# VectorE and ScalarE as loops over one ring of rows, in a fused linear layer with a low-rank part

## The chip, the cores and the metric

The kernel runs on one core of a Trainium2 chip. The metric is the device time of one execution in microseconds (us), the median of several runs. A separate execution was profiled; its trace gives the durations below.

## The reference

`x` is 16 x 2048 rows of 256 float32 values, 32768 rows in all. The result is a linear layer plus a scaled low-rank one:

```python
x_flat = x.reshape(-1, in_dim)              # 32768 x 256
y = x_flat @ W                              # W: 256 x 256
lora_out = ((x_flat @ lora_A) * lora_E) @ lora_B   # rank 16
y = y + scale * lora_out                    # float32, 32768 x 256
```

Input and output have 33.5 MB each.

## The kernel before

**Weights.** The low-rank part is folded into the weights once: `weff = W + A diag(E) B * scale`, in bf16. This takes two small transposes (L194), two small products (L198), and four short VectorE instructions (L127 to L138). After that, the work is one 256 x 256 product for every row of `x`.

**Chunks.** The rows are cut by `PLAN` into chunks; a plan entry `b` means `b` rows on each of the 128 partitions. Before, there are nine chunks: 16, seven times 32, and 16. A chunk of 32 is a DMA of 4 MB, in which each partition gets one run of 32 KB. Six buffers `xy` of 32 rows each hold chunks; the result is written over the input in the same buffer and stored from there. Together they take 192 KB of each partition.

**Steps.** Each chunk is worked on in steps of `Q = 4` rows a partition, 64 steps in all:

- VectorE rounds four rows to bf16 (`xb`, L146).
- TensorE transposes them with eight transposes into PSUM (`ps_xt`, L176).
- VectorE copies the transposed block to SBUF (`xt`, L155).
- TensorE multiplies: eight matmuls into PSUM (`ps_y`, L184).
- ScalarE copies the result to `xy` in float32 (L163). At the end of a chunk a drain (L165) adds one to the semaphore `s_rdy`.

`xb`, `xt`, `ps_xt` and `ps_y` have two buffers each. VectorE and TensorE run one step ahead: the rounding and the transposes of step k+1 come before the copy and the products of step k. TensorE's program is a loop of two steps already; its waits take semaphores down by one (`take`, L170). The programs of VectorE and ScalarE are written out for all 64 steps, with a wait for `s_in[i]` on VectorE at the first step of chunk i.

**Transfers.** All large transfers are issued by SP, in one queue (q1), and are split over 16 DMA engines. The order is written out by hand: the weights, six loads (`LEAD`), then for each chunk a wait for `s_rdy` and its store (L109). After the store of chunk 2, `AFTER` puts the loads of chunks 6, 7 and 8 (L102), each behind a wait until the store from the same buffer has landed (`s_out`). At the end SP waits for the last stores.

Of the kernel before, what the change touches and what calls it, by code (L numbers as in the profile page):

```python
# [6 lines left out]

PLAN = [16] + [32] * 7 + [16]  # L10

ROWS, SLOTS = 32, 6

LEAD = 6
AFTER = {2: [6, 7, 8]}

Q = 4


@with_exitstack  # L20
def kernel(
    ctx: ExitStack,
    tc: tile.TileContext,
    x: bass.AP,
    W: bass.AP,
    lora_A: bass.AP,
    lora_B: bass.AP,
    lora_E: bass.AP,
    scale: bass.AP,
    out: bass.AP,  # L30
):
    nc = tc.nc
    P = 128
    FP32 = mybir.dt.float32
    BF16 = mybir.dt.bfloat16

    x_flat = x.flatten_outer_dims()
    out_flat = out.flatten_outer_dims()
    N, K = x_flat.shape
    M = out_flat.shape[1]  # L40
    R = lora_B.shape[0]
    KC = K // P
    CHUNKS = len(PLAN)
    assert K == M and sum(PLAN) * P == N and all(b % Q == 0 for b in PLAN)

    def sbuf(name, shape, dt):
        return ctx.enter_context(nc.sbuf_tensor(name, shape, dt))

    def psum(name, shape, dt):
        return ctx.enter_context(nc.psum_tensor(name, shape, dt))  # L50

    xy = [sbuf(f"xy{s}", [P, ROWS, K], FP32) for s in range(SLOTS)]
    xb = [sbuf(f"xb{s}", [P, Q, K], BF16) for s in range(2)]
    xt = [sbuf(f"xt{s}", [P, Q, KC, P], BF16) for s in range(2)]
    w_sb = sbuf("w_sb", [P, KC, M], FP32)
    a_sb = sbuf("a_sb", [P, KC, R], FP32)
    b_sb = sbuf("b_sb", [R, M], FP32)
    e_sb = sbuf("e_sb", [R, 1], FP32)
    b_bf = sbuf("b_bf", [R, M], BF16)
    ate = sbuf("ate", [R, KC, P], BF16)  # L60
    weff = sbuf("weff", [P, KC, M], BF16)
    ident = sbuf("ident", [P, P], FP32)
    ident_bf = sbuf("ident_bf", [P, P], BF16)

    ps_xt = [psum(f"ps_xt{s}", [P, Q, KC, P], BF16) for s in range(2)]
    ps_y = [psum(f"ps_y{s}", [P, Q, M], FP32) for s in range(2)]
    ps_at = psum("ps_at", [P, KC, P], FP32)
    ps_aeb = psum("ps_aeb", [P, KC, M], FP32)

    sem = tc.alloc_semaphore  # L70
    s_w, s_a, s_b, s_e = sem("s_w"), sem("s_a"), sem("s_b"), sem("s_e")
    s_in = [sem(f"s_in{i}") for i in range(CHUNKS)]

    again = CHUNKS - SLOTS
    s_out = [sem(f"s_out{i}") for i in range(again + 1)]
    s_id = sem("s_id")
    s_lora = sem("s_lora")
    s_lpe = sem("s_lpe")
    s_xb = sem("s_xb")
    s_t = sem("s_t")  # L80
    s_xt = sem("s_xt")
    s_p = sem("s_p")
    s_y = sem("s_y")
    s_rdy = sem("s_rdy")

    starts = [sum(PLAN[:i]) * P for i in range(CHUNKS)]

    def rows_of(flat, i):
        b, r0 = PLAN[i], starts[i]
        return flat[r0:r0 + b * P, :].rearrange("(p b) k -> p b k", b=b)  # L90


    steps = [(i, r) for i, b in enumerate(PLAN) for r in range(0, b, Q)]
    n = len(steps)
    assert n % 2 == 0

    with tc.tile_critical(sync_engine=mybir.EngineType.SP, no_gpsimd_drain=True):  # L97
        sp, pe, dve, act, pool = nc.sync, nc.tensor, nc.vector, nc.scalar, nc.gpsimd


        def load(i):
            sp.dma_start(out=xy[i % SLOTS][:, :PLAN[i], :], in_=rows_of(x_flat, i)).then_inc(s_in[i], 16)  # L102

        sp.dma_start(out=w_sb[:], in_=W.rearrange("(c p) m -> p c m", p=P)).then_inc(s_w, 16)
        for i in range(LEAD):
            load(i)
        for i in range(CHUNKS):
            sp.wait_ge(s_rdy, i + 1)
            sp.dma_start(out=rows_of(out_flat, i), in_=xy[i % SLOTS][:, :PLAN[i], :]).then_inc(s_out[min(i, again)], 16)  # L109
            for later in AFTER.get(i, []):  # L110
                if later >= SLOTS:
                    sp.wait_ge(s_out[later - SLOTS], 16)
                load(later)
        for i in range(len(s_out) - 1):
            sp.wait_ge(s_out[i], 16)


        pool.memset(ident[:], 0.0).then_inc(s_id, 1)  # L118
        pool.wait_ge(s_id, 1)
        pool.affine_select(  # L120
            out=ident[:], in_=ident[:], compare_op=mybir.AluOpType.not_equal, fill=1.0,
            base=0, pattern=[[-1, P]], channel_multiplier=1,
        ).then_inc(s_id, 1)


        dve.wait_ge(s_id, 2)
        dve.tensor_copy(out=ident_bf[:], in_=ident[:]).then_inc(s_lora, 1)  # L127
        dve.wait_ge(s_b, 16)
        dve.tensor_copy(out=b_bf[:], in_=b_sb[:]).then_inc(s_lora, 1)  # L129
        dve.wait_ge(s_e, 16)  # L130
        dve.wait_ge(s_lpe, 1)
        dve.tensor_scalar(  # L132
            out=ate[:], in0=ps_at[:R, :, :], scalar1=e_sb[:], scalar2=float(scale),
            op0=mybir.AluOpType.mult, op1=mybir.AluOpType.mult,
        ).then_inc(s_lora, 1)
        dve.wait_ge(s_w, 16)
        dve.wait_ge(s_lpe, 2)
        dve.tensor_add(out=weff[:], in0=w_sb[:], in1=ps_aeb[:]).then_inc(s_lora, 1)  # L138

        def round_step(k):  # L140
            i, r = steps[k]
            if r == 0:
                dve.wait_ge(s_in[i], 16)
            if k >= 2:
                dve.wait_ge(s_t, k - 1)
            dve.tensor_copy(out=xb[k % 2][:], in_=xy[i % SLOTS][:, r:r + Q, :]).then_inc(s_xb, 1)  # L146

        round_step(0)
        for k in range(n):
            if k + 1 < n:  # L150
                round_step(k + 1)
            dve.wait_ge(s_t, k + 1)
            if k >= 2:
                dve.wait_ge(s_p, k - 1)
            dve.tensor_copy(out=xt[k % 2][:], in_=ps_xt[k % 2][:]).then_inc(s_xt, 1)  # L155


        act.dma_start(out=a_sb[:], in_=lora_A.rearrange("(c p) r -> p c r", p=P)).then_inc(s_a, 16)
        act.dma_start(out=b_sb[:], in_=lora_B).then_inc(s_b, 16)
        act.dma_start(out=e_sb[:], in_=lora_E[:, None]).then_inc(s_e, 16)  # L160
        for k, (i, r) in enumerate(steps):
            act.wait_ge(s_p, k + 1)
            act.copy(out=xy[i % SLOTS][:, r:r + Q, :], in_=ps_y[k % 2][:]).then_inc(s_y, 1)  # L163
            if r + Q == PLAN[i]:
                act.drain().then_inc(s_rdy, 1)  # L165

        def take(s):
            pe.wait_ge(s, 1).then_inc(s, -1)  # L170

        def transposes(k):
            take(s_xb)
            for j in range(Q):
                for c in range(KC):
                    t = pe.transpose(ps_xt[k % 2][:, j, c, :], xb[k % 2][:, j, c * P:(c + 1) * P], ident_bf[:])  # L176
            t.then_inc(s_t, 1)

        def products(k):
            take(s_xt)  # L180
            take(s_y)
            for j in range(Q):
                for c in range(KC):
                    m = pe.matmul(  # L184
                        ps_y[k % 2][:, j, :], xt[k % 2][:, j, c, :], weff[:, c, :],
                        start=(c == 0), stop=(c == KC - 1),
                    )
            m.then_inc(s_p, 1)

        pe.sem_inc(s_y, 2)  # L190
        pe.wait_ge(s_a, 16)
        pe.wait_ge(s_id, 2)
        for c in range(KC):
            t = pe.transpose(ps_at[:R, c, :], a_sb[:, c, :], ident[:])  # L194
        t.then_inc(s_lpe, 1)
        pe.wait_ge(s_lora, 3)
        for c in range(KC):
            m = pe.matmul(ps_aeb[:, c, :], ate[:, c, :], b_bf[:], start=True, stop=True)  # L198
        m.then_inc(s_lpe, 1)
        transposes(0)  # L200
        pe.wait_ge(s_lora, 4)
        with pe.Fori(0, n // 2 - 1):
            transposes(1)
            products(0)
            transposes(0)
            products(1)
        transposes(1)
        products(0)
        products(1)


    with tc.tile_critical(sync_engine=mybir.EngineType.SP, no_gpsimd_drain=True):
        nc.sync.wait_ge(s_out[again], 16 * (CHUNKS - again))
# [34 lines left out]
```

## Time and profile before

| | us |
|---|---|
| median of 3 runs | 165.41 (165.13 to 165.42) |
| the profiled execution's own time | 165.19 |
| its span, first to last instruction | 163.4 |
| TensorE busy | 90.8 |
| VectorE busy | 84.1 |
| ScalarE busy | 66.1 |
| DMA, mean over the span | 413 GB/s |

The profiled execution's time has 1.8 us around its span. The page lists groups of instructions by line, with the total busy time, the mean of one in nanoseconds, and the idle time just before them with what ended it. Times in the trace count from the start of the span. In the list of DMA issues, the time to landing counts from the issue, so it holds the time in the queue too: a store of 4 MB takes 39.5 us at the median. Where the prediction speaks of single packets, these are the trace's records of the DMA engines: when a packet began, how long it took, its size and queue. A landing is the moment at which one of the 16 DMA engines has reported its part of a transfer.

### The profile page before, as it was taken

To read this page: it belongs to the slowest core of one execution; us is meant where nothing else is said; L and a number is where in the kernel's file an instruction comes from. 1 tells how busy PE (TensorE), PEld (TensorE's weight loads), DVE (VectorE), ACT (ScalarE), POOL (GpSimd) and SP (SyncE) were. 2 spreads that over 40 slices of the span, in tenths; PEclk is the share of its full clock that TensorE was granted. 3 is DMA by queue.
4 is the path that set the end of the run, shared out by engine and by line. 5 is a ranking of instruction groups with operands and counts; after the bars stand their busy time and mean duration, and the time that the engine had idled before them with its cause. 6 is when DMAs were issued, how large, how long until landed. Compare 5 with 4: busy or idle time off the path is not lost. (4 is left out here: it accounts for less than half of the span.)

```text
span 163.4 us, 2684 instructions
## 1 busy us (share of the span) xinstructions
PE 90.8 (56%) x1028; PEld 81.6 (50%) x1028; DVE 84.1 (51%) x132; ACT 66.1 (40%) x65; POOL 0.7 (0%) x6
## 2 busy tenths in 40 slices
PE   0169499999999999990000099999992000000000
PEld 0047389999999999980000089999981000000000
DVE  0165299999999999950000169999970000000000
ACT  3002447777777777772000026777774000000000
POOL 1000000000000000000000000000000000000000
PEclk9999999999999999999555559999999755555555
DMA  4999999899999999999999998999999999999990
GB/s 133 421 433 489 393 449 449 385 473 425 403 481 393 385 409 481 393 457 425 433 433 425 441 441 383 465 437 425 425 435 433 441 409 465 417 425 441 409 409 32
DMA packets 3203, 67.43 MB, mean 413 GB/s; under 512 B 624, under 2 KB 896, under 8 KB 896
## 3 DMA queue, kind: packets, MB, share of 16 engines
q1 hardware_dynamic: 2864, 67.37, 96.4%
q10 hardware_dynamic: 336, 0.03, 0.3%
q14 instruction: 3, 0.02, 0.0%
HBM read 33.85 MB, written 33.55 MB: 412 GB/s over the span
## 5 line engine op out<-in xcount | busy, mean ns | idle before, releaser
L163 ACT COPY xy<-ps_y 128x1024 f32<-128x1024 f32 x64 | 64.8, 1013 | 56.2 <-PE ps_y L184 56.2
L184 PE MATMUL ps_y<-weff,xt 128*128 128x256 bf16 x512 | 68.6, 278 | 0.5 <-PEq L170 0.3
L146 DVE CAST xb<-xy 128x1024 bf16<-128x1024 f32 x64 | 43.6, 683 | 24.9 <-DMA xy<-in_x_dram 24.9
L176 PE MATMUL ps_xt<-ident_bf,xb 128*128 128x128 bf16 x512 | 40.9, 226 | 24.7 <-PEq L170 24.7
L184 PEld LDWEIGHTS ps_y<-weff,xt 128*128 128x128 bf16 x512 | 48.4, 100 | 6.4 <-issue 1.1
L176 PEld LDWEIGHTS ps_xt<-ident_bf,xb 128*128 128x128 bf16 x512 | 35.5, 102 | 27.3 <-issue 25.7
L155 DVE COPY xt<-ps_xt 128x1024 bf16<-128x1024 bf16 x64 | 44.2, 691 | 5.4 <-PE ps_xt L176 3.7
L194 PE MATMUL ps_at<-ident,a_sb 128*16 128x128 f32 x2 | 0.6, 402 | 4.1 <-DMA a_sb<-in_lora_A_dram 4.1
L198 PE MATMUL ps_aeb<-b_bf,ate 16*128 16x256 bf16 x2 | 0.6, 404 | 3.6 <-DVE ate L132 3.6
L129 DVE CAST b_bf<-b_sb 16x256 bf16<-16x256 f32 x1 | 0.3, 280 | 3.9 <-DMA b_sb<-in_lora_B_dram 3.9
L163 ACT ACT_TABLE_LOAD x1 | 1.3, 1283 | 2.5 <-issue 2.5
L198 PEld LDWEIGHTS ps_aeb<-b_bf,ate 16*128 16x128 bf16 x2 | 0.1, 106 | 4.1 <-DVE ate L132 4.1
L194 PEld LDWEIGHTS ps_at<-ident,a_sb 128*16 128x16 f32 x2 | 0.1, 94 | 4.1 <-DMA a_sb<-in_lora_A_dram 4.1
L132 DVE TENSOR_SCALAR ate<-ps_at,e_sb 16x256 bf16<-16x256 f32 x1 | 0.5, 472 | 1.6 <-DMA e_sb<-in_lora_E_dram 1.6
L127 DVE CAST ident_bf<-ident 128x128 bf16<-128x128 f32 x1 | 0.2, 227 | 1.7 <-POOL ident L120 1.7
L138 DVE TENSOR_TENSOR weff<-w_sb,ps_aeb 128x512 bf16<-128x512 f32 x1 | 0.7, 687 | 0.8 <-PE ps_aeb L198 0.8
L120 POOL TENSOR_SCALAR_AFFINE_SELECT ident<-ident 128x128 f32<-128x128 f32 x1 | 0.3, 293 | 0.2 <-POOL ident L118 0.2
L118 POOL MEMSET ident<- 128x128 f32 x1 | 0.2, 204 | 0.5 <-SPq L97 0.5
L229 POOL MEMSET const-bfloat16-1.0<- 128x1 bf16 x1 | 0.1, 101 | 0.0
L229 POOL MEMSET const-uint8-127<- 128x1 uint8 x1 | 0.1, 101 | 0.0
L229 POOL MEMSET const-float32-0.0<- 128x1 f32 x1 | 0.1, 98 | 0.2 <-issue 0.2
L229 POOL MEMSET const-float32-1.0<- 128x1 f32 x1 | 0.1, 98 | 0.0
## 6 DMA issues: line engine op xcount, KB each, us to landing
xy<-in_x_dram SPq DMA_DIRECT2D x7, 4096.0 KB, 29.1
out_dram<-xy SPq DMA_DIRECT2D x7, 4096.0 KB, 39.5
xy<-in_x_dram SPq DMA_DIRECT2D x2, 2048.0 KB, 16.3
out_dram<-xy SPq DMA_DIRECT2D x2, 2048.0 KB, 39.3
w_sb<-in_W_dram SPq DMA_DIRECT2D x1, 256.0 KB, 2.9
a_sb<-in_lora_A_dram ACTq DMA_DIRECT2D x1, 16.0 KB, 3.1
b_sb<-in_lora_B_dram ACTq DMA_DIRECT2D x1, 16.0 KB, 4.4
e_sb<-in_lora_E_dram ACTq DMA_DIRECT2D x1, 0.1 KB, 5.7
```

The lines of the kernel that those rows point to most:

```text
L120: pool.affine_select(out=ident[:], in_=ident[:], compare_op=mybir.AluOpType.not_equal, fill=1.0, base=0, pattern=[[-1, P]], channel_multip ...
L129: dve.tensor_copy(out=b_bf[:], in_=b_sb[:]).then_inc(s_lora, 1)
L132: dve.tensor_scalar(out=ate[:], in0=ps_at[:R, :, :], scalar1=e_sb[:], scalar2=float(scale), op0=mybir.AluOpType.mult, op1=mybir.AluOpType. ...
L138: dve.tensor_add(out=weff[:], in0=w_sb[:], in1=ps_aeb[:]).then_inc(s_lora, 1)
L146: dve.tensor_copy(out=xb[k % 2][:], in_=xy[i % SLOTS][:, r:r + Q, :]).then_inc(s_xb, 1)
L155: dve.tensor_copy(out=xt[k % 2][:], in_=ps_xt[k % 2][:]).then_inc(s_xt, 1)
L163: act.copy(out=xy[i % SLOTS][:, r:r + Q, :], in_=ps_y[k % 2][:]).then_inc(s_y, 1)
L176: t = pe.transpose(ps_xt[k % 2][:, j, c, :], xb[k % 2][:, j, c * P:(c + 1) * P], ident_bf[:])
L184: m = pe.matmul(ps_y[k % 2][:, j, :], xt[k % 2][:, j, c, :], weff[:, c, :], start=(c == 0), stop=(c == KC - 1),)
L194: t = pe.transpose(ps_at[:R, c, :], a_sb[:, c, :], ident[:])
L198: m = pe.matmul(ps_aeb[:, c, :], ate[:, c, :], b_bf[:], start=True, stop=True)
L229: nc = _bacc.Bacc("TRN2", target_bir_lowering=False, num_devices=1)
```

## The change

- `xy` is one tensor of 192 rows (`RING`). A view `xy_turns` divides it into turns of eight rows (`TURN`), and each turn into two steps of four.
- VectorE's and ScalarE's programs are loops over turns. They pass over the ring twice: 24 turns in a first loop, the remaining 8 in a second one, with the ring's rows addressed by a register.
- VectorE no longer waits for `s_in`. GpSimd waits for each load in turn and adds its four turns to the semaphore `s_ld`; VectorE takes one for each turn.
- Within a turn the order is: both roundings, then both copies on VectorE; both transposes, then both products on TensorE. The step ahead across turns is gone, and TensorE's loop has 32 turns with nothing before or after it.
- ScalarE drains once a turn, and SP's waits for `s_rdy` count turns.
- The plan is eight chunks of 32 rows. Six loads go first; after the store of chunk 1 come the loads of chunks 6 and 7, which wait for the stores of the chunks whose rows they take (0 and 1).

The diff, cut to its core:

```diff
-PLAN = [16] + [32] * 7 + [16]
-ROWS, SLOTS = 32, 6
+PLAN = [32] * 8
+RING = 192
 LEAD = 6
-AFTER = {2: [6, 7, 8]}
+AFTER = {1: [6, 7]}
 Q = 4
+TURN = 2 * Q
...
-    xy = [sbuf(f"xy{s}", [P, ROWS, K], FP32) for s in range(SLOTS)]
+    xy = sbuf("xy", [P, RING, K], FP32)
+    xy_turns = xy[:].rearrange("p (t k q) d -> p t k (q d)", k=2, q=Q)
...
+    passes = [RING, sum(PLAN) - RING]
+    turns = sum(PLAN) // TURN
...
         for i in range(CHUNKS):
-            sp.wait_ge(s_rdy, i + 1)
-            sp.dma_start(out=rows_of(out_flat, i), in_=xy[i % SLOTS][:, :PLAN[i], :]).then_inc(s_out[min(i, again)], 16)
+            sp.wait_ge(s_rdy, (starts[i] + PLAN[i]) // TURN)
+            sp.dma_start(out=rows_of(out_flat, i), in_=ring_of(i)).then_inc(s_out[min(i, again)], 16)
             for later in AFTER.get(i, []):
-                if later >= SLOTS:
-                    sp.wait_ge(s_out[later - SLOTS], 16)
+                sp.wait_ge(s_out[owner[later]], 16)
                 load(later)
...
+        for i in range(CHUNKS):
+            pool.wait_ge(s_in[i], 16).then_inc(s_ld, PLAN[i] // TURN)
+
+        def take(engine, s):
+            engine.wait_ge(s, 1).then_inc(s, -1)
...
-        round_step(0)
-        for k in range(n):
-            if k + 1 < n:
-                round_step(k + 1)
-            dve.wait_ge(s_t, k + 1)
-            if k >= 2:
-                dve.wait_ge(s_p, k - 1)
-            dve.tensor_copy(out=xt[k % 2][:], in_=ps_xt[k % 2][:]).then_inc(s_xt, 1)
+        for rows in passes:
+            with dve.Fori(0, rows // TURN) as turn:
+                take(dve, s_ld)
+                for k in range(2):
+                    dve.tensor_copy(out=xb[k][:], in_=xy_turns[:, bass.ds(turn, 1), k, :]).then_inc(s_xb, 1)
+                for k in range(2):
+                    take(dve, s_t)
+                    dve.tensor_copy(out=xt[k][:], in_=ps_xt[k][:]).then_inc(s_xt, 1)
...
-        for k, (i, r) in enumerate(steps):
-            act.wait_ge(s_p, k + 1)
-            act.copy(out=xy[i % SLOTS][:, r:r + Q, :], in_=ps_y[k % 2][:]).then_inc(s_y, 1)
-            if r + Q == PLAN[i]:
+        for rows in passes:
+            with act.Fori(0, rows // TURN) as turn:
+                for k in range(2):
+                    take(act, s_p)
+                    act.copy(out=xy_turns[:, bass.ds(turn, 1), k, :], in_=ps_y[k][:]).then_inc(s_y, 1)
                 act.drain().then_inc(s_rdy, 1)
...
-        transposes(0)
         pe.wait_ge(s_lora, 4)
-        with pe.Fori(0, n // 2 - 1):
+        with pe.Fori(0, turns):
+            transposes(0)
             transposes(1)
             products(0)
-            transposes(0)
             products(1)
-        transposes(1)
-        products(0)
-        products(1)
```

## The prediction

> **What bounds the kernel now.** First the busy line, the slices and the queue table of the page.
>
> ```profile
> PE 90.8 (56%) x1028; PEld 81.6 (50%) x1028; DVE 84.1 (51%) x132; ACT 66.1 (40%) x65; POOL 0.7 (0%) x6
> ...
> DMA  4999999899999999999999998999999999999990
> ...
> q1 hardware_dynamic: 2864, 67.37, 96.4%
> q10 hardware_dynamic: 336, 0.03, 0.3%
> q14 instruction: 3, 0.02, 0.0%
> ```
>
> No compute engine passes 56%; the 16 DMA engines are full from the second slice to the last but one. Next the timeline of SP's issues (start, time to the last issue's end, what): the stream is never starved.
>
> ```profile
> 1.43 3.15 SPq L102 DMA_DIRECT2D xy<-in_x_dram  x6
> 22.99 21.45 SPq L109 DMA_DIRECT2D out_dram<-xy  x3
> 64.30 19.69 SPq L102 DMA_DIRECT2D xy<-in_x_dram  x3
> 84.04 41.08 SPq L109 DMA_DIRECT2D out_dram<-xy  x6
> ```
>
> Then the chain of waits in order of time (start, us, what); these are its last pieces, and nothing computes after them.
>
> ```profile
> 122.64 1.05 PE ps_y L184 x8
> ...
> 123.71 1.01 ACT xy L163
> ```
>
> ScalarE ends at 124.7 us, the last store is issued at 124.8 and lands at 162.1; SP only waits in between. So the end is the DMA stream's. Next I took every q1 packet of the trace (start, duration, size) and joined each to the DMA engine whose previous packet ended there. Each engine moves 112 packets of 32 KB (1.213 us each, the commonest value) and 32 of 16 KB (0.611 us) back to back: 112 x 1.213 + 32 x 0.611 = 155.4 us of floor after a start at 3.2 to 3.6. Fourteen engines end their last packet between 159.15 and 160.09. Two end at 161.65 and 161.73, and these two set the time: their landings are at 162.10 and 162.11, the 14th's is at 160.43. The span's last 1.3 us follow the last landing.
>
> Why are two late? **Straggler A** carries instruction fetches. The three q14 packets (8 KB each) start at 41.41, 101.64 and 118.69. On A the queue pauses 0.30 us at 41.4 and the next packet takes 0.65 too long; at 118.7 again, 0.30 and 0.36: 1.61 us in all. The fetch at 101.64 costs another engine 0.66, which still ends at 159.83 and decides nothing. Whose fetches are they? VectorE has executed 71 recorded instructions at the first and 201 at the third, 130 apart, and 8 KB is 128 instructions of 64 bytes (8192 / 128); ScalarE is at 60 at the second. TensorE, whose loop branches back 31 times, shows none. **Straggler B** has no fetch. Its store packets take about 0.1 us too long, one after another, from 59 to 72 and from 106 to 125 us: exactly while stores run and the engines compute (25 half-turns of ScalarE copies). It loses some 2.4 us, and nothing while loads run.
>
> **The change, part by part.**
>
> *Loops in VectorE and ScalarE.* The built programs shrink from 217 to 46 instructions (VectorE) and 90 to 40 (ScalarE). Both end before the counts (71, 60) at which the first fetch came, so all three q14 packets should go. On A this takes away 0.60 of pauses and 1.01 of long packets: -1.61 us. A rule speaks against loops: the Trainium skill, "Runtime: NRT & Kernel Launch", section "Instruction fetch mechanics", says that a taken branch outside the two resident pages forces a fetch by DMA, and that kernels therefore prefer unrolling. If it struck here, there would be one fetch or more per turn. This trace has a loop of 31 taken branches and three fetches in all, none tied to them; the sum goes by the trace.
>
> *Eight chunks of 32 rows.* 128 packets of 1.213 = 155.26 for 155.41: -0.14 us on each engine; one load and one store fewer, each ending in a semaphore packet of 9 ns: -0.02. A without its fetches: 161.73 - 1.61 - 0.16 = 159.96; the next engine in the list, 160.09 - 0.16 = 159.93, agrees. So if B is not late, the last packet ends 1.77 us earlier.
>
> *Order of transfers.* Loads 0 to 5 are now 24 MB (before 22), then stores 0 and 1, loads 6 and 7, stores 2 to 7; four blocks in one direction, as before. From landings (first load 9.53 us before; eight 32 KB packets instead of 16 KB ones add 4.81) chunk 0 is in at 14.4 and every later DMA takes 9.71: loads end at 62.9, store 0 72.6, store 1 82.3, load 6 92.1, load 7 101.8; store 7 would begin at 150.3. Load 6 is issued when store 0 has landed (72.6), with store 1 (9.7 us) still queued; load 7 at 82.4 with load 6 queued; stores 2 and 3 follow at once. Never less than 9.7 us of work is queued, where an issue needs 1.7 us to its first packet (1.43 to 3.15). Cost: nothing, and if that cover went, 1.7 us per gap.
>
> *GpSimd's turns.* It had nothing to do after 1.7 us. Its wait stands between a landing and VectorE: two semaphore hops for one. In the trace VectorE's cast starts 0.02 us after the second load's landing (19.24 to 19.26), so a second hop is a few hundredths, at most the 0.3 us with which a waiting copy starts on ScalarE; for eight chunks at most 2.4 us of the cover below. Nothing is queued behind it but its own later waits. Off the path.
>
> *The compute loop.* It may be slower at no cost as long as store 7 is ready when the queue reaches it (150.3, less 1.7 for the issue: 148.5). The steady pace before is two steps of 1.32 us per 8 rows. The groups of the page that a turn is made of (busy, mean ns of one, idle time before):
>
> ```profile
> L163 ACT COPY xy<-ps_y 128x1024 f32<-128x1024 f32 x64 | 64.8, 1013 | 56.2 <-PE ps_y L184 56.2
> ...
> L146 DVE CAST xb<-xy 128x1024 bf16<-128x1024 f32 x64 | 43.6, 683 | 24.9 <-DMA xy<-in_x_dram 24.9
> ...
> L155 DVE COPY xt<-ps_xt 128x1024 bf16<-128x1024 bf16 x64 | 44.2, 691 | 5.4 <-PE ps_xt L176 3.7
> ...
> L163 ACT ACT_TABLE_LOAD x1 | 1.3, 1283 | 2.5 <-issue 2.5
> ```
>
> VectorE and TensorE no longer run one step ahead across a turn. From the timeline: transposes 0.61, xt copy 0.69, then 0.28 to the first product, two product blocks at 0.87, with the second transposes beside them: about 3.4 us per turn of 8 rows. On ScalarE the built program has the table load *inside* the first loop, after the wait for the first product: 24 times 1.28 us. A turn there is 1.28 + 2 x 1.01 + loop end and waits. The latter have no row on ScalarE; TensorE's loop end is 0.27 (0.036 + 0.208 and gaps) and a copy behind a wait starts 0.31 late. Bounds: 3.4 us (TensorE's pace, all hidden) to 1.28 + 2.03 + 0.62 + 1.04 (the drain counted in full) = 5.0. I take 4.1, since the drain's record lies beside the copy (1.04 against 1.01) and the second wait is over by then. Chunk 0 in at 14.4, one slow turn at the half clock (+1.8), 24 x 4.1 = 98.4, 8 x 3.4 = 27.2: chunk 7 is ready at 141.8, 6.7 us before it is needed; stores 0 to 6 have more. The limit for a turn is (148.5 - 27.2 - 16.2) / 24 = 4.38.
>
> On that table load the skill has a harsher price ("ScalarE: Activation LUTs", "What ACT_TABLE_LOAD costs": about 1.28 and a drain of 1.38 per switch); by it a turn would be 5.5 us and the kernel some 26 us later. The one load in this trace shows 1.283 and no drain behind it.
>
> Sum: 165.19 (profiled execution; span 163.4 and 1.8 around it) - 1.77 = 163.4; it is 0.22 under the median of the runs, so 165.41 - 1.77 = **163.6**; I say 163.7 for the engine that may come next.
>
> **The rivals.** (1) *Straggler B stays.* If its long packets occur in every run, and are not an effect of recording instructions, B is the end. Stores over compute grow: stores 0 and 1 (62.9 to 82.3, 9.5 half-turns) and from 101.8 on (20): 29.5 for 25, at 0.1 us each +0.45, less 0.16: 165.41 + 0.2 = 165.6; range 165.1 to 166. For it: B's loss is in the trace. Against: it follows the compute instructions, on one engine, and only in transfers to HBM, as records written there would. The trace can't decide.
> (2) *ScalarE's turn exceeds 4.38 us* because of the table load in its loop: slower. Each 0.1 us beyond adds 24 x 0.1 = 2.4 us. At 5.0 chunk 7 is ready at 163.4, 15 us late: about 178. For it: the load is in the loop and my 0.7 us of loop end and waits is an estimate. Against: 6.7 us of cover.
> (3) *The change doesn't do what it says:* a loop that lies across a page still fetches. With two or three fetches 165.2; with one per turn on one engine at 0.66, tens of us more. TensorE's loop speaks against it.
>
> **How the numbers follow.** Forecast 0.52 (own range 163.2 to 164.6); rival 1 0.20, of which 0.03 faster, 0.12 within the bound and 0.05 slower; rival 2 0.18; rival 3 0.06, half within the bound; 0.04 for a loss that I have not seen. The bound is 0.2%, 0.33 us, about what this measurement can tell from no change. Faster 0.52 + 0.03 = 0.55, same 0.12 + 0.03 = 0.15, slower 0.30. The range goes from 163.2 over rival 1 to 166.4; rival 2 and the bad half of 3 lie above it.
>
> **What would show it.** Right: q14 absent from the queue table, DMA full to the end, ScalarE's table load x24 with turns near 4.1 us and its last copy near 142, SP's last store issued before 148. In the profiled run B may still be the last landing; then the span falls less than the times do. Wrong: q14 packets that come back each turn; a hole in the DMA slices before the last store; times at 165.6 with B's packets long.

## The result and the profile after

The changed kernel takes 166.82 us (median of 4 runs, 166.76 to 167.13) against 165.32 us before: ratio 1.0096, 95% interval 1.0079 to 1.0114. It is 1.5 us slower where 1.8 us less was forecast. Its profiled execution, the slowest of the four, took 167.13 us, with a span of 165.3.

First the page of the changed kernel: busy line, slices of the clock and the DMA engines, queue table.

```profile
PE 94.4 (57%) x1028; PEld 79.2 (48%) x1028; DVE 81.6 (49%) x132; ACT 92.5 (56%) x88; POOL 0.7 (0%) x6
...
PEclk9999999999999999999999999999999999555555
DMA  6999999989999999999999998999999999999940
...
q1 hardware_dynamic: 2576, 67.37, 95.5%
q10 hardware_dynamic: 336, 0.03, 0.2%
```

The q14 row is gone: no instruction was fetched by DMA within the span. The DMA engines are full up to the last two slices; these read 4 and 0 where before only the last was thin (9 and 0). So something still moves at the end, but little of the 16 engines: few of them are at work.

The timeline of SP's issues in the changed kernel:

```profile
0.94 0.44 SPq L116 DMA_DIRECT2D w_sb<-in_W_dram  x1
1.43 2.87 SPq L114 DMA_DIRECT2D xy<-in_x_dram  x6
34.45 15.37 SPq L121 DMA_DIRECT2D out_dram<-xy  x2
73.44 10.70 SPq L114 DMA_DIRECT2D xy<-in_x_dram  x2
84.19 52.58 SPq L121 DMA_DIRECT2D out_dram<-xy  x6
```

The last store is issued at 136.8 us, well before its turn in the queue near 150. The stream was not starved by the compute. The last pieces of the chain of waits say the same; the compute ends at 136.4 (ACTq is ScalarE's sequencer; L176 is the drain).

```profile
134.44 0.73 ACT xy L175
135.17 0.06 issue
135.23 0.05 ACTq L175
135.28 0.06 issue
135.33 1.04 ACTq L176
```

The time is in one DMA engine. The landing records of the trace have, for each large DMA, 16 entries, one for each DMA engine (us, changed kernel):

| DMA | 14th of 16 | 15th | last |
|---|---|---|---|
| load 5 | 63.18 | 63.21 | 63.33 |
| store 0 | 72.91 | 73.02 | 73.43 |
| store 1 | 82.87 | 82.91 | 83.79 |
| load 7 | 102.01 | 102.12 | 103.68 |
| store 2 | 111.73 | 111.81 | 114.10 |
| store 3 | 121.38 | 121.46 | 124.52 |
| store 4 | 131.04 | 131.16 | 134.91 |
| store 7 | 160.02 | 160.19 | 164.04 |

Fifteen DMA engines are done at 160.19 us. The prediction had its straggler A land at about that time once its fetches were gone (its last packet at 159.96, and landings come 0.38 later). The 16th falls back with each store as long as the engines compute, and stays 3.8 us behind from 135 on. Straggler B is alone now, and it is later than before (164.04 for 162.10).

The theory for the experiments, **"records"**: each instruction that any engine executes (and that is recorded in the trace) delays one DMA engine a little while that engine stores. I counted the trace's instruction records, control instructions too, inside the windows of stores, and summed what the packets there took too long (those 0.03 to 0.2 us over the common value):

| kernel | records in stores | excess, us | ns each |
|---|---|---|---|
| before | 442 + 498 = 940 | 2.36 | 2.5 |
| changed | 502 + 898 = 1400 | 3.31 | 2.4 |

The rivals: **"work"**, in which the compute engines' memory traffic slows that DMA engine; **"order"**, in which the plan of chunks and the order of transfers cost the time; **"slow engine"**, in which it stores slower whatever else runs; and "ScalarE's turn", rival 2 of the prediction. The experiments ran in several jobs, and each job timed the kernel before as well: its median lay between 165.32 and 165.84 us, so a ratio compares times of one job.

### The profile page after: what moved, and what is told of

Read it like the earlier page. It is cut to its first block, busy times and chain, and to the rows that moved or that the text cites. A ratio compares the mean times of both kernels' runs of the same rounds, so it can differ in the third digit from the quotient of the medians.

```text
span 165.3 us, 3152 instructions
## 1 busy us (share of the span) xinstructions
PE 94.4 (57%) x1028; PEld 79.2 (48%) x1028; DVE 81.6 (49%) x132; ACT 92.5 (56%) x88; POOL 0.7 (0%) x6
## 5 line engine op out<-in xcount | busy, mean ns | idle before, releaser
L191 PE MATMUL ps_y<-weff,xt 128*128 128x256 bf16 x512 | 63.6, 276 | 26.8 <-PEq L139 26.8
L175 ACT COPY xy<-ps_y 128x1024 f32 x64 | 61.7, 1015 | 11.7 <-ACTq L139 11.5
L191 PEld LDWEIGHTS ps_y<-weff,xt 128*128 128x128 bf16 x512 | 46.9, 98 | 40.0 <-issue 31.5
L165 DVE COPY xt<-ps_xt 128x1024 bf16<-128x1024 bf16 x64 | 41.3, 686 | 39.3 <-DVEq L139 39.3
L175 ACT ACT_TABLE_LOAD x24 | 30.8, 1283 | 32.2 <-ACTq L139 32.2
L162 DVE CAST xb<-xy 128x1024 bf16 x64 | 41.1, 685 | 3.2 <-DVEq L139 3.2
L183 PE MATMUL ps_xt<-ident_bf,xb 128*128 128x128 bf16 x512 | 34.7, 222 | 4.8 <-PEq L139 4.8
L183 PEld LDWEIGHTS ps_xt<-ident_bf,xb 128*128 128x128 bf16 x512 | 32.0, 99 | 6.1 <-issue 5.3
```

What stands on the lines that cost most here:

```text
L162: dve.tensor_copy(out=xb[k][:], in_=xy_turns[:, bass.ds(turn, 1), k, :]).then_inc(s_xb, 1)
L165: dve.tensor_copy(out=xt[k][:], in_=ps_xt[k][:]).then_inc(s_xt, 1)
L175: act.copy(out=xy_turns[:, bass.ds(turn, 1), k, :], in_=ps_y[k][:]).then_inc(s_y, 1)
L183: t = pe.transpose(ps_xt[k][:, j, c, :], xb[k][:, j, c * P:(c + 1) * P], ident_bf[:])
L191: m = pe.matmul(ps_y[k][:, j, :], xt[k][:, j, c, :], weff[:, c, :], start=(c == 0), stop=(c == KC - 1),)
```

## The experiments

### The plan alone

```diff
 (kernel before)
-PLAN = [16] + [32] * 7 + [16]
+PLAN = [32] * 8
-AFTER = {2: [6, 7, 8]}
+AFTER = {1: [6, 7]}
```

> The kernel before with eight chunks of 32 rows and two late loads; VectorE's and ScalarE's programs stay written out. Theory 'records' (each recorded instruction, of whatever engine, costs one DMA engine about 2.5 ns while it stores): about as many instructions as before fall on stores (22 to 25 steps of 41), the three instruction fetches stay, so 165.1 us, within 0.3 of before. Rival 'order' (the chunk plan or the order of transfers is what costs the time): about 166.8 us, as with the whole change.

165.91 us against 165.84 in the same job: ratio 1.0003 (0.9989 to 1.0018). Plan and order cost nothing; "order" is out. Both stragglers are there, landing last at 162.83 and 162.85, and three fetches stand in the queue table (here of this kernel's page):

```profile
q14 instruction: 3, 0.02, 0.0%
```

### Instructions without data

```diff
 (changed kernel)
+RECORDS = {5: 14, 7: 38}
 for i in range(CHUNKS):
     pool.wait_ge(s_in[i], 16).then_inc(s_ld, PLAN[i] // TURN)
+    if i in RECORDS:
+        with pool.Fori(0, RECORDS[i]):
+            for _ in range(8):
+                pool.sem_inc(s_x, 1)
+                take(pool, s_x)
```

> The changed kernel; GpSimd, idle there, runs small loops of semaphore instructions from the landing of load 5 and from that of load 7 on, about 930 instructions that move no data. Theory 'records': the late DMA engine loses 930 x 2.5 ns = 2.3 us more, time about 169.1 us. Rival 'work' (the memory traffic of the compute engines slows that DMA engine): 166.8 us, no change.

170.33 us against 165.84: ratio 1.027 (1.0253 to 1.0287). It is slower by more than was expected. The last landing is at 166.96, 6.83 us behind the 15th (3.85 without the added instructions): 2.98 us for the added 938 records, 3.2 ns each. "Work" can't explain these 2.98 us: the added instructions name no tile. Some 30 of them ran past store 1, beside load 6; the price hardly changes by that.

### The stream without row work, and with instructions beside it

The changed kernel without rounding, transposes, products and copies of rows; GpSimd tells SP of each landing. Then the same with GpSimd's loops.

> The changed kernel without its row work (no rounding, transposes, products and copies; the input is stored as it came), with the same order of transfers. Both 'records' and 'work' expect no long store packets and a last landing like that of the other 15 DMA engines, 160.2: time 166.8 - 3.8 = 163.0 us. Rival 'slow engine' (one DMA engine stores slower by itself): 166.8 us.

163.41 us (ratio 0.9859, 0.9842 to 0.9875). All 16 engines' last landings lie between 159.48 and 159.92. "Slow engine" is out, and this is what the stream costs.

> The same without row work, with GpSimd's 930 semaphore instructions beside the stores. 'Records': one DMA engine is late by 930 x 2.5 ns = 2.3 us, time about 165.3 us. 'Work': as without them, about 163.0 us.

167.94 us (ratio 1.0131, 1.0114 to 1.0148), more than "records" said. The last landing, 163.02, is 2.8 us behind the 15th (160.21), half a microsecond more than the 2.3 expected; and GpSimd's second loop ran past that landing and held up the end of the kernel itself, which is the rest. So it was run again with fewer rounds:

```diff
-RECORDS = {5: 14, 7: 38}
+RECORDS = {5: 14, 7: 30}
```

> The stream without row work, with GpSimd's loops beside the stores again, the second one shortened to 30 rounds so that GpSimd is done before the last landing; about 790 instructions. 'Records' at 3.0 ns each (the landing of the run with 938 was 2.8 us late): 2.4 us more than the stream alone, 165.8 us. 'Work': 163.4.

165.82 us in a job where before took 165.69 (ratio 1.0014, 1.0000 to 1.0028). The busy line of this run's page shows how little else there is:

```profile
span 163.9 us, 910 instructions
...
PE 1.2 (1%) x4; PEld 0.2 (0%) x4; DVE 1.7 (1%) x4; POOL 0.7 (0%) x6
...
DMA  6999998998999998998999999999899899998960
```

With nearly no work and 787 records inside the store windows it takes as long as the whole kernel before. Its last landing, 162.20, is 2.4 us behind the 15th. A further rival is that only semaphore instructions count. The traces speak against it: in the same windows there are 686 of them here, 98 in the kernel before and 169 in the changed one, so the delays would be 3.5, 24 and 20 ns each, where the price by all records is 3.0, 2.5 and 2.4. Last, the same kind of instructions beside loads:

```diff
-RECORDS = {5: 14, 7: 30}
+RECORDS = {0: 26, 6: 4}
```

> The same stream with about 540 such instructions placed beside loads instead (26 rounds after load 0, 4 after load 6) and none beside stores. 'Records', as it cost nothing in the loads of the kernel before: 163.4 us, as the stream alone. Rival 'any transfer' (each instruction costs 3.0 ns whatever moves): 1.6 us more, 165.0.

163.47 us in the same job (ratio 0.9874, 0.9848 to 0.9901): as the stream alone. The 474 and 74 records beside loads cost nothing.

```profile
span 161.6 us, 658 instructions
...
DMA  5999999999999999999999999999999999999993
```

The DMA slices are full to the end again, with no thin tail.

### Two stragglers, two cures

If A (VectorE's fetches) and B (instructions beside stores) end together in the kernel before, curing one alone must bring nothing. A pause on VectorE keeps instructions away from stores 0 to 2; loops take the fetches away. The loops here are one step ahead as the written-out program is, on VectorE alone; ScalarE stays written out.

```diff
 (kernel before: the pause)
+PAUSE = 32
 for k in range(n):
+    if k + 1 == PAUSE:
+        dve.wait_ge(s_out[2], 16)
     if k + 1 < n:
         round_step(k + 1)
```

> The kernel before, with one wait added on VectorE: before step 32 of 64 it waits until the third store has landed, so that fewer steps fall on stores (14 instead of 25). 'Records': the DMA engine that the instructions slow is early by about 1 us, but the one with VectorE's two instruction fetches stays at 161.7, so no gain: within 0.3 us of before. 'Work' says the same. A rival that takes only the first straggler for real expects a gain of 0.5 us or more; one that takes the compute for the bound expects a loss, as it ends later.

```diff
 (kernel before: VectorE as loops; xy is one tensor of 192 rows, chunk 0 in rows 16 to 31,
  GpSimd hands out s_ld as in the changed kernel)
+def turns_of(start, stop):
+    with dve.Fori(start, stop) as turn:
+        round_step(now, bass.ds(turn, 1), 1)
+        copy_step(0)
+        round_step(ahead, bass.ds(turn, 1), 0)    # first step of the next turn
+        copy_step(1)
...
+round_step(now, slice(head, head + 1), 0)
+turns_of(head, whole - 1)
+last_turn(whole - 1, 0)
+turns_of(0, rest - 1)
+last_turn(rest - 1, None)
```

> The kernel before with VectorE's program alone as loops, still one step ahead, nine chunks and the old order; ScalarE stays written out. 'Records': VectorE's two fetches go, but the other straggler stays and gets 3.5 instructions a step more: 25 x 44.5 x 2.6 ns = 2.9 us lost instead of 2.5, so 0 to 0.5 us slower than before. Forecast of the prediction (fetches alone decide): 1.6 us faster.

```diff
 (both: against the loops alone)
-turns_of(head, whole - 1)
+turns_of(head, head + PAUSE)          # PAUSE = 16 turns
+dve.wait_ge(s_out[2], 16)
+turns_of(head + PAUSE, whole - 1)
```

> Both: VectorE as loops one step ahead, and the pause until the third store has landed. 'Records': no fetch on the first straggler, 14 x 44.5 x 2.6 ns = 1.6 us lost on the second; its last packet ends near 160.9 instead of 161.7: 0.6 to 1.2 us faster than before. Without the second straggler's mechanism it would be as fast as the loops alone.

| kernel (before: 165.74 us) | us | ratio, 95% interval | last two landings | records in stores |
|---|---|---|---|---|
| pause alone | 165.73 | 1.0010 (0.9993 to 1.0026) | 161.74, 162.46 | 688 |
| loops alone | 166.19 | 1.0018 (1.0004 to 1.0032) | 160.57, 163.16 | 1010 |
| both | 165.12 | 0.9958 (0.9944 to 0.9972) | 160.33, 161.90 | 738 |

With the pause alone the last engine is A: it was 1.5 us behind the 15th already when the last load landed (108.47 for 106.92), before any store beside compute. Each alone brings no gain, the loops a small loss; together they are 0.6 us faster than before and beat both kernels. The loops alone bring the 15th engine to 160.57, near the forecast's 160.3, and the kernel is not faster for it. In the list of waits of the kernel with both (us in total, times, longest) the pause is the fourth by length:

```profile
DVE xb L157 <- DMA out_dram<-xy: 24.0, 1, 24.0
```

And from its page, TensorE's slices and the fetches in the queue table:

```profile
PE   0259299999999980000049999999999500000000
...
q14 instruction: 1, 0.01, 0.0%
```

One fetch is left (by its time, 108.4, ScalarE's), on an engine with slack. The hole in TensorE's row is the pause, and the busy stretches lie over the first six and the last three loads; what runs on past 107 us, over stores, is the 1.6 us that B is still late.

### The table load out of ScalarE's loop

```diff
 (changed kernel)
+act.wait_ge(s_id, 2)
+act.copy(out=warm[:], in_=ident[:, :1])
 for rows in passes:
     with act.Fori(0, rows // TURN) as turn:
```

> The changed kernel with one short ScalarE copy ahead of its loops, so that the activation table is loaded once and not in each of 24 turns. 'Records': a turn of the first loop falls from 3.76 to about 3.5 us, the compute ends some 6 us sooner, about 160 fewer instructions fall on stores: 0.4 us less than the changed kernel, 1.0 to 1.2 us over before. Rival (ScalarE's turn sets the end): several us faster than the changed kernel.

166.83 us against 165.74: ratio 1.0062 (1.0039 to 1.0085). The changed kernel's ratio was 1.0096 (1.0079 to 1.0114); the two were taken in different jobs and their intervals touch, so the 0.34% between them (0.6 us) is not beyond doubt. In the traces it is as expected: 1259 records in stores for 1400, and the slow engine 3.44 us behind the 15th for 3.85. ScalarE's turns, from the timeline of the changed kernel (start, us, what, idle before):

```profile
98.77 1.28 ACT L175 ACT_TABLE_LOAD   x1 [0.53 <-ACTq L139]
100.06 1.93 ACT L175 COPY xy<-ps_y 128x1024 f32 x2
102.52 1.28 ACT L175 ACT_TABLE_LOAD   x1 [0.53 <-ACTq L139]
103.82 1.93 ACT L175 COPY xy<-ps_y 128x1024 f32 x2
```

And from the timeline of the kernel with the table loaded once:

```profile
99.98 1.93 ACT L178 COPY xy<-ps_y 128x1024 f32 x2 [1.56 <-ACTq L140]
103.47 1.93 ACT L178 COPY xy<-ps_y 128x1024 f32 x2 [1.57 <-ACTq L140]
```

A turn is 3.75 us with the load and 3.49 without, where ScalarE waits 1.57 for products. The load costs 0.26 a turn and not 1.28, and it did not set the end.

## Why the prediction was wrong

- **What bounds the kernel: right.** The DMA stream, and in it the slowest of 16 DMA engines. Two of them ended together, A with two fetches and B with long store packets. All later runs fit that picture.
- **Loops take the fetches away: right in kind and size.** No q14 packet in the changed kernel; loops of 24, 8 and 32 turns fetched nothing. The 15th landing is at 160.19; the sum gave 159.96 + 0.38 = 160.3. The Trainium skill's rule on taken branches ("Runtime: NRT & Kernel Launch", "Instruction fetch mechanics") had no case here: none of the loops fetched. Rival 3 is out.
- **The choice between the forecast and rival 1: this is the step that failed.** The sum took A's 1.61 us off and put B's delay at nothing. The text said that the trace can't decide whether B's long packets occur in every run, and then gave the forecast 0.52 and rival 1 0.20, on the argument that B's loss might be an effect of recording instructions. Whatever its cause, it is in the runs that are timed: 787 records without data add 2.4 us to the times of the bare stream (165.82 us; 163.47 in the same job with the instructions beside loads). With B in the times, taking A away can't bring anything: the changed kernel ends with B's landing at 164.04, 3.85 us behind the 15th. An engine that is as late as the one cured is the next bound, and it was in the same list.
- **The size of rival 1: too small by more than a microsecond.** It counted half-turns at 0.1 us, 29.5 for 25, which gave +0.45 and 165.6 us (less 0.16 that is +0.29, written as 0.2; it changes little). The number of half-turns was about right, but the cost goes by instructions. Loops add control instructions: VectorE has 400 records for 212, ScalarE 357 for 85. In stores there are 1400 for 940, and the excess is 3.31 for 2.36 us: +0.95. B's last landing moved by 1.94, and so did the profiled times (165.19 to 167.13); the medians are 1.5 apart. One single load packet at 100.28 us took 0.65 too long, and the slow engine's distance from the 15th grew from 1.10 to 1.56 us in that load; such packets show near the end of load 7 in the kernel with the table loaded once (0.76 too long; lag 1.62) and with the plan alone (0.58 and 0.78) as well, while the longest there in the bare stream is 0.21. What makes it, and the rest of the 1.94, was not separated.
- **The compute loop: safe, as said.** A turn took 3.75 us in the first pass (4.1 taken) and 3.49 in the second (3.4 taken); the last copy ended at 136.4 for a limit of 148.5. The slow first turn came as well: its products took 3.56 us, those of the next turn 1.91. One reading was wrong and cost nothing: the 0.31 us of idle time before ScalarE's copies is no late start but the wait for the products, as the shown chain tells (they end at 122.64 + 1.05 = 123.69, the copy starts at 123.71). Rival 2 is out. The harsh price for a table load ("ScalarE: Activation LUTs", "What ACT_TABLE_LOAD costs") did not apply: the row shows 1283 ns with the copy right behind it.
- **Packets and order: right.** -0.16 us was too small to see, and the plan alone measured 1.0003.
- **GpSimd's turns:** off the path, as said. GpSimd cost time only where an experiment gave it loops beside the stores.

## What to carry to other kernels

Where a kernel is bound by the DMA stream, list the last landing of each DMA engine and ask what makes the late ones late: with two stragglers of different cause at the same time, a change that cures one is worth nothing until the other is cured too. A loss that stands in the trace belongs in the forecast, whatever it is thought to come from, since the timed runs may have it as well. Count instructions, control instructions included, and not steps or work, where a cost falls on whoever shares a path with them; and, as far as these runs go, place compute beside loads rather than beside stores.

## What the runs showed of the hardware

- In these runs each executed instruction, even a semaphore instruction on GpSimd that moves no data, delays the stores of one DMA engine: 2.4 to 2.5 ns in the kernel before and the changed one, and 3.0 to 3.2 ns for GpSimd's; why the two prices differ is open. Beside loads it costs nothing (548 instructions, 163.47 us for 163.41). All runs here, the timed ones too, list a span and a granted clock; whether the delay exists where nothing is recorded was not tried, so that it comes from the recording is not shown.
- An instruction fetch of 8 KB, itself 0.31 us, costs the DMA engine that carries it 0.66 to 0.95 us when its queue is full.
- At the first turn from loads to stores most DMA engines have one or two long packets, 2 to 4 us before the last load lands, also with no compute at all (0.44 us a DMA engine on average in the bare stream, 0.28 with instructions beside its loads, 0.9 in the changed kernel).
- TensorE's granted clock stayed at full speed (1.00 in windows from 10 to 135 us) throughout the compute in the changed kernel, with gaps of up to 0.9 us before products; even so the products of the first turn took 3.56 us, those of the next 1.91.
